# Two one-element PSUM tiles taken ahead of the first head products of an encoder kernel

## The chip, the cores and the metric

The kernel runs on one core of a Trainium2 chip, in one launch. The metric is the device time of one execution in microseconds, the median of several runs. Times inside an execution come from one profiled execution and are counted from its first instruction.

## The reference

Two layers of a bidirectional encoder on 1024 tokens of width 1024, everything in float32. Layer 0 mixes tokens by latent attention, layer 1 by dilated windows; each layer ends with a squared-ReLU MLP. What matters here is the start of layer 0:

```python
def mla_mixer(h, pos, w_in, g_qa, w_qb, g_kva, w_kvb, g_q, g_k, w_o):
    proj = h @ w_in                                   # 1024 -> 384 + 256 + 32
    q_lat = proj[..., :Q_LORA]
    kv_lat = proj[..., Q_LORA:Q_LORA + KV_LORA]
    k_rope = rope(proj[..., Q_LORA + KV_LORA:], pos)
    q = (rms_norm(q_lat, g_qa) @ w_qb).reshape(B, S, MLA_HEADS, MLA_QK)
    kv = (rms_norm(kv_lat, g_kva) @ w_kvb).reshape(B, S, MLA_HEADS, MLA_NOPE + MLA_V)
    ...
    q = rms_norm(q, g_q)
    k = rms_norm(k, g_k)
    o = dense_attention(q, k, v, MLA_QK ** -0.5)
    return o.reshape(B, S, MLA_HEADS * MLA_V) @ w_o
```

## The kernel before

Every float32 product is made of three matmuls on a high and a low part of each operand (`mm3`, L423 to L427). PSUM has 8 banks, and each PSUM tile here fills one bank. PSUM tiles come from pools; a pool is opened for a stage and closed after it, and the next pool takes over the same 8 banks. A tile may be written once the last reader of the tile that held its bank before has finished; this is kept bank by bank (`reuse_waits="tile"`), so a new stage may begin in the free banks while the old stage still reads others. Which bank a tile gets is settled when the program is built. So is the order of each engine's instructions: each engine works through its own list in that order, and waits on semaphores that count what the other engines have finished.

Function `mla` uses three such pools one after the other.

- **`psA`** (L566): the input projection, for eight token tiles `t` of 128 rows. Accumulators `psin` of two kinds: tag `q`, 416 columns (L588, banks 2 to 5), and tag `kv`, which holds two token tiles (banks 6 and 7). `latent(t)` (L594) reads them: two squares on ACT (L597, L598), `rstd` (ACT L112 and L113, DVE L114 to L116), two scalings on DVE (L600, L601) and a copy of the rotary columns `krw` on ACT (L602). `latents` (L605) transposes the latents on PE into `pslt` (banks 0 and 1) and splits them on ACT and DVE (L121, L122) into `latT`. `k_rope` (L620) ends the stage: DVE L623 and L624, and six POOL instructions.
- **`psB`** (L768): the head products, over two halves `hf` of eight heads and eight token tiles `t`. Per step, two tiles `pq` (9 matmuls of 384 columns each) and two `pkv` (6 matmuls of 512 columns each), then squares on ACT (`sq` L791, `sk`, in the trace `sqk`, L793), sums on DVE (L795, L796), `rstd`, scalings into `st` (ACT L801, DVE L802 and L805, POOL L807 and the rope), and a store to DRAM (`qkv`, L814). In the first half the transposes still owed, `pslt`, stand between the steps (L817 to L822). In the second half the first two heads are prepared between the steps: `prep` (transposes `pqk`; the last of them is split by ACT L733 and DVE L734), `rowmax` (matmul `pmx`, DVE maximum L756) and `rowstore` (`pmt`).
- **`psC`** (L840): the attention itself. Tag `s` (`pss`, L853 to L855) has banks 0 to 2, tag `t` (`pmx` and others) banks 3 to 5, tag `av` banks 6 and 7.

Of the kernel before, what the change touches and what calls it, by code (L numbers as in the profile page):

```python
# [41 lines left out]
class K:  # L42
# [496 lines left out]
    def mla(self, xs, ada0, xs1, mods, tail):  # L539


        nc, a, tc = self.nc, self.a, self.tc
# [225 lines left out]
        with tc.tile_pool(name="psB", bufs=8, space=PSUM, reuse_waits="tile") as psp:  # L768
            B = lambda name: psp.tile([P, 512], F32, tag="b", name=self.nm(name))
            raw = None  # L770
            for hf in range(2):
                w = hw[hf]
                for t in range(NT):
# [1629 lines left out]
```

## Time and profile before

| | us |
|---|---|
| runs, median (lowest to highest) | 3236.82 (3232.02 to 3237.32) |
| the profiled execution's own time | 3228.74 |
| its span, first to last instruction | 3227.0 |

The profile gives each engine's busy time (PE is the matmul engine, DVE and ACT the vector and scalar engines, POOL a slower vector engine, SP issues transfers), what an idle engine waited for, and each instruction's start and length. In a timeline row the first number is the start, the second the length, and a bracket gives the idle time ahead of it and what ended it. Matmuls are pipelined, so the length of one overlaps the next: the distance from start to start is what a matmul costs. The granted clock is the share of full speed that PE got. Here the head products stand from 111 to 230 us of the span.

### The profile page before, as it was taken

How to read it: one execution, taken by the hardware profiler on the slowest of the kernel's cores; microseconds unless marked ns; L12 is line 12 of the kernel's file. 1: busy time of each engine (PE TensorE's matmuls, PEld its weight loads, DVE VectorE, ACT ScalarE, POOL GpSimd, SP SyncE). 2: the span in 40 equal slices, each digit the busy share in tenths (PEclk: the TensorE clock that was granted, in tenths of full speed). 3: DMA queues.
4: the chain of work that ended last, by engine and by line, in shares of the span. 5: the costliest groups of instructions: out<-in, count | busy, mean ns of one | idle time of the engine just before them, and what ended most of it. 6: DMA issues, size and time to landing. Idle time of an engine off the chain costs nothing. (4 is left out here: it accounts for less than half of the span.)

```text
span 3227.0 us, 50801 instructions
## 1 busy us (share of the span) xinstructions
PE 3127.3 (97%) x18034; PEld 2645.7 (82%) x18034; DVE 2383.3 (74%) x4243; ACT 1733.2 (54%) x3507; POOL 919.4 (28%) x1226
## 2 busy tenths in 40 slices
PE   6999999999999999989999999999999999999999
PEld 6877677778788788877889999998998888887887
DVE  6677777746987776588757778777888588778566
ACT  5547777754554433543226677667665264444332
POOL 7464556530111100000123445444454001110010
PEclk9999999999999999999999999999999999999999
DMA  5352322253555779544638877888778536448554
GB/s 193 121 190 80 108 84 92 70 167 111 177 200 175 268 220 307 179 148 162 224 125 187 184 179 178 191 190 174 173 165 202 167 106 214 150 152 311 204 190 129
DMA packets 538926, 552.31 MB, mean 171 GB/s; under 512 B 199429, under 2 KB 421042, under 8 KB 538666
## 3 DMA queue, kind: packets, MB, share of 16 engines
q1 hardware_dynamic: 500874, 443.00, 48.4%
q0 software_dynamic: 27360, 91.31, 7.6%
q10 hardware_dynamic: 10432, 14.68, 1.6%
q8 instruction: 144, 2.36, 0.3%
q14 instruction: 116, 0.95, 0.1%
HBM read 376.17 MB, written 132.62 MB: 158 GB/s over the span
## 5 line engine op out<-in xcount | busy, mean ns | idle before, releaser
L426 PE MATMUL psm<-dl,dh 128*128 128x512 f32 x896 | 350.7, 391 | 8.3 <-DVE dl L122 8.2
L425 PE MATMUL psm<-hf,wf 128*128 128x512 f32 x896 | 350.4, 391 | 2.6 <-ACT wf L121 2.6
L426 PE MATMUL psm<-hf,wf 128*128 128x512 f32 x896 | 349.7, 390 | 0.0
L427 PE MATMUL psm<-dh,dl 128*128 128x512 f32 x896 | 349.7, 390 | 0.0
L427 PE MATMUL psm<-hf,wf 128*128 128x512 f32 x896 | 347.2, 390 | 0.4 <-DVE wf L122 0.4
L425 PE MATMUL psm<-dh,dh 128*128 128x512 f32 x896 | 335.9, 392 | 5.2 <-ACT dh L121 5.2
L425 PE MATMUL psproj<-wqkh,hTp 128*128 128x256 f32 x1024 | 302.0, 295 | 0.0
L427 PE MATMUL psproj<-wqkh,hTp 128*128 128x256 f32 x1024 | 290.4, 284 | 0.0
L426 PE MATMUL psproj<-wqkl,hTp 128*128 128x256 f32 x1024 | 290.3, 283 | 0.0
L121 ACT ACTIVATE dh<-ufr 128x1024 fp32r<-128x1024 f32 x112 | 118.3, 1056 | 175.3 <-PE psm L427 50.0
L426 PEld LDWEIGHTS psm<-dl,dh 128*128 128x128 f32 x896 | 168.7, 188 | 46.5 <-DVE dl L122 11.6
L425 PEld LDWEIGHTS psproj<-wqkh,hTp 128*128 128x128 f32 x1024 | 196.6, 192 | 8.5 <-issue 0.4
L425 PEld LDWEIGHTS psm<-dh,dh 128*128 128x128 f32 x896 | 168.5, 189 | 42.7 <-ACT dh L121 7.8
L425 PEld LDWEIGHTS psm<-hf,wf 128*128 128x128 f32 x896 | 168.7, 188 | 40.1 <-ACT wf L121 5.5
L427 PEld LDWEIGHTS psm<-hf,wf 128*128 128x128 f32 x896 | 168.5, 188 | 35.8 <-DVE wf L122 1.2
L426 PEld LDWEIGHTS psm<-hf,wf 128*128 128x128 f32 x896 | 168.7, 188 | 35.0
L427 PEld LDWEIGHTS psm<-dh,dl 128*128 128x128 f32 x896 | 168.8, 188 | 34.6
L426 PEld LDWEIGHTS psproj<-wqkl,hTp 128*128 128x128 f32 x1024 | 196.8, 192 | 0.2 <-DVE wqkl L122 0.2
L427 PEld LDWEIGHTS psproj<-wqkh,hTp 128*128 128x128 f32 x1024 | 196.4, 192 | 0.2
L122 DVE TENSOR_TENSOR dl<-ufr,dh 128x1024 fp32r<-128x1024 f32 x112 | 136.9, 1222 | 77.3 <-ACT dh L121 58.6
L756 DVE TENSOR_REDUCE mx<-pmx 128x1 f32<-128x512 f32 x256 | 165.1, 682 | 29.5 <-PE pmx L754 29.3
L122 POOL TENSOR_TENSOR pl<-p,ph 128x1024 fp32r<-128x1024 f32 x58 | 141.3, 2436 | 138.8 <-ACT ph L121 133.8
(400 smaller groups left out, 8926.4 us busy)
## 6 DMA issues: line engine op xcount, KB each, us to landing
ufr<-uf SPq DMA_DIRECT2D x112, 512.0 KB
adaw<-in_ada_w SPq DMA_DIRECT2D x96, 512.0 KB
w2r<-in_mlp_w SPq DMA_DIRECT2D x96, 512.0 KB
w1r<-in_mlp_w SPq DMA_DIRECT2D x64, 512.0 KB
bt<-bias SPq DMA_DIRECT2D x128, 256.0 KB
wqkr<-in_dil_w_in SPq DMA_DIRECT2D x96, 256.0 KB
qkv<-st SPq DMA_DIRECT2D x32, 512.0 KB
hraw<-qkv SPq DMA_DIRECT2D x32, 512.0 KB
```

The source lines that it names most:

```text
L121: nc.scalar.activation(hi, src, AF.Copy)
L122: (lo_eng or nc.vector).tensor_tensor(lo, src, hi.bitcast(F32), op=ALU.subtract)
L425: mm(out, lh, rh, start=first, stop=False)
L426: mm(out, lh, rl, start=False, stop=False)
L427: mm(out, ll, rh, start=False, stop=last)
L756: nc.vector.tensor_reduce(maxes[h][:, 2 * j + b : 2 * j + b + 1], ps, op=ALU.max, axis=AX.X)
```

## The change

Ahead of the loops of the second stage, two tiles are taken from its pool and one element of each is set to zero by DVE. Nothing reads them. They take the first two banks that the builder hands out, and the products get later ones.

```diff
         with tc.tile_pool(name="psB", bufs=8, space=PSUM, reuse_waits="tile") as psp:
             B = lambda name: psp.tile([P, 512], F32, tag="b", name=self.nm(name))
             raw = None
+            for _ in range(2):
+                nc.vector.memset(B("skip")[0:1, 0:1], 0.0)
             for hf in range(2):
                 w = hw[hf]
                 for t in range(NT):
```

Lines behind it have numbers higher by 2 in the changed kernel (L791 becomes L793). The banks that the builder hands out in the second stage, in the order in which tiles are taken:

| tile | before | after | what held the bank of after in `psA` |
|---|---|---|---|
| the two `skip` | | 0, 7 | `pslt`; `kv` of `t` 6 and 7 |
| `pq`, `pq` of `t` 0 | 0, 7 | 6, 5 | `kv` of `t` 4 and 5; `q` of `t` 5 |
| `pkv`, `pkv` of `t` 0 | 6, 5 | 4, 1 | `q` of `t` 6; `pslt` |
| `pslt`, `pslt` | 4, 3 | 2, 3 | `q` of `t` 4; `q` of `t` 7 |
| `pq`, `pq` of `t` 1 | 2, 1 | 0, 7 | the two `skip` |
| ... | | | |
| `pq`, `pq`, `pkv`, `pkv` of the last step | 3, 7, 1, 4 | 3, 5, 7, 2 | |
| the last `pqk` | 2 | 0 | |

From the first `pq` to the last `pqk` the banks of after are those of before with the numbers exchanged (0, 1, 2, 3, 4, 5, 6, 7 become 6, 7, 0, 3, 2, 1, 4, 5): two tiles that shared a bank before share one now. All other pools have the banks they had, and all tiles in SBUF their addresses.

The order of the instructions on PE, ACT, POOL and SP is the same. On DVE the two memsets stand between the two instructions of the last `k_rope`; the first rows are before, the second after.

```order
L601 TENSOR_SCALAR lat_7109<-psin_6956,lry_7112 128x256
L623 TENSOR_TENSOR krsq_7123<-krw 128x128
L624 TENSOR_REDUCE krss<-krsq_7123 128x4
L795 TENSOR_REDUCE hms_7182<-sq_7180 128x8
L796 TENSOR_REDUCE hms_7182<-sqk_7181 128x8
```

```order
L601 TENSOR_SCALAR lat_7109<-psin_6956,lry_7112 128x256
L623 TENSOR_TENSOR krsq_7123<-krw 128x128
L772 MEMSET skip_7144 1x1
L772 MEMSET skip_7146 1x1
L624 TENSOR_REDUCE krss<-krsq_7123 128x4
L797 TENSOR_REDUCE hms_7186<-sq_7184 128x8
L798 TENSOR_REDUCE hms_7186<-sqk_7185 128x8
```

The memsets are behind the scaling L601 of the last `latent`, and so behind the last reader of both their banks. In the dilated attention of layer 1, one DVE instruction of a `rstd` (`drt`, L114) also stands two rows earlier than before; nothing else differs on DVE.

What PE waits for differs at both ends of the stage. At its beginning, with the semaphores that a row waits for in brackets, before and then after:

```order
L427 MATMUL pq_7144<-whh_7015,latT_6774 128x384
L425 MATMUL pq_7145<-whh_6983,latT_6743 128x384 [waits DVE_49]
L426 MATMUL pq_7145<-whl_6984,latT_6743 128x384
...
L425 MATMUL pkv_7146<-whh_7031,latT_6773 128x512 [waits Activation_49]
L426 MATMUL pkv_7146<-whl_7032,latT_6773 128x512
```

```order
L427 MATMUL pq_7148<-whh_7015,latT_6774 128x384
L425 MATMUL pq_7149<-whh_6983,latT_6743 128x384 [waits PE_49,Activation_49]
L426 MATMUL pq_7149<-whl_6984,latT_6743 128x384
...
L425 MATMUL pkv_7150<-whh_7031,latT_6773 128x512 [waits Activation_49]
L426 MATMUL pkv_7150<-whl_7032,latT_6773 128x512
```

Before, the second `pq` waits for DVE's last scaling L601 of `t` 7, which reads bank 7. After, it waits for ACT's copy L602 of `t` 5, and the first `pkv` for the copy L602 of `t` 6.

At the end of the stage, the first scores of the attention, before and then after:

```order
L853 MATMUL pss_8696<-qh_8131,kh_8129 128x512 [waits DMAHW4_49,DMAHW3_49,DVE_49]
L854 MATMUL pss_8696<-ql_8132,kh_8129 128x512
L855 MATMUL pss_8696<-qh_8131,kl_8130 128x512
L754 MATMUL pmx_8701<-kh_8359,qh_8361 128x512 [waits DVE_49,Activation_49]
L853 MATMUL pss_8697<-qh_8131,kh_8129 128x512 [waits PE_49]
```

```order
L855 MATMUL pss_8700<-qh_8135,kh_8133 128x512 [waits DMAHW4_49,DMAHW3_49,DVE_49]
L856 MATMUL pss_8700<-ql_8136,kh_8133 128x512
L857 MATMUL pss_8700<-qh_8135,kl_8134 128x512
L754 MATMUL pmx_8705<-kh_8363,qh_8365 128x512 [waits DVE_49,Activation_49]
L855 MATMUL pss_8701<-qh_8135,kh_8133 128x512 [waits DVE_49,Activation_49]
```

The first `pss` (bank 0) now waits for DVE L734, which reads the last `pqk`; the second (bank 2) for the last scaling L805 of the stage (L807 of the changed kernel) and ACT's copy beside it. The `pmx` between them (bank 3) waits for the same scaling L802 as before.

## The prediction

> **What bounds the kernel now.** I read the busy times first, then what PE waited for in the whole execution. In a wait row the figures are the total in us, how often, and the longest.
>
> ```profile
> PE 3127.3 (97%) x18034; PEld 2645.7 (82%) x18034; DVE 2383.3 (74%) x4243; ACT 1733.2 (54%) x3507; POOL 919.4 (28%) x1226
> PE pq L425 <- DVE lat L601: 4.0, 1, 4.0
> PE pmt L762 <- DVE nm L761: 2.6, 1, 2.6
> PE pmx L754 <- DVE st L802: 2.3, 1, 2.3
> PE pq L425 <- DVE st L802: 0.9, 1, 0.9
> ```
>
> PE is busy for 97% of the span, so a time that PE loses anywhere is lost at the end, and a stall removed is a gain unless a later wait takes it back. The change touches the banks of one stage, and the first wait row is the one place where that stage waits for the stage before it: one wait of 4.0 us. The other three lie inside the stage or at its end. PE's timeline there:
>
> ```profile
> 111.16 0.34 PE L425 MATMUL pq<-whh,latT 128*128 128x384 f32 x1
> 112.55 0.34 PE L427 MATMUL pq<-whh,latT 128*128 128x384 f32 x1
> 116.86 0.69 PE L425 MATMUL pq<-whh,latT 128*128 128x384 f32 x1 [3.97 <-DVE lat L601]
> 119.88 0.39 PE L425 MATMUL pkv<-whh,latT 128*128 128x512 f32 x1
> 122.65 0.82 PE L612 MATMUL pslt<-ident,lat 128*128 128x128 f32 x6
> 123.22 0.42 PE L425 MATMUL pq<-whh,latT 128*128 128x384 f32 x1
> ```
>
> The first `pq` runs through. The second, in bank 7, stands 3.97 us until DVE has read that bank for the last time. Then its nine matmuls take 119.88 - 116.86 = 3.02 us. The nine of the first `pq` took 1.39 us from the first start to the ninth, 0.174 us each or 1.57 us in all: another 1.45 us is lost. The granted clock says why; in a row of this view it stands behind the engines' busy times, and ahead of the transfers' share and their GB/s:
>
> ```profile
> 112.00:120.00 8.00, 4.03 (x16) 3.71 (x15) 3.46 (x12) 2.59 (x11) 1.79 (x6) 0.79 0.00 0
> 117.00:118.00 1.00, 1.00 (x4) 1.00 (x5) 0.29 (x1) 0.02 (x1) 1.00 (x5) 0.50 0.00 0
> ```
>
> After the stall PE runs at half clock. And there is no transfer between 112 and 120 us. So no queue of transfers carries over the stall, and every later transfer is issued by work behind it.
>
> **The change, part by part.** What the new banks wait for, and what ACT and DVE do meanwhile:
>
> ```profile
> 113.74 0.20 ACT L602 ACTIVATE krw<-psin 128x32 f32<-128x32 f32 x1 [0.87 <-DVE lat L600]
> 116.54 0.48 ACT L791 ACTIVATE sq<-pq 128x384 f32<-128x384 f32 x1
> 121.47 0.39 ACT L793 ACTIVATE sqk<-pkv 128x256 f32<-128x256 f32 x1 [0.90 <-PE pkv L427]
> 121.75 0.38 ACT L801 ACTIVATE st<-pkv 128x256 f32<-128x256 f32 x1
> 122.85 0.38 ACT L793 ACTIVATE sqk<-pkv 128x256 f32<-128x256 f32 x1 [0.72 <-PE pkv L427]
> 125.09 0.49 ACT L791 ACTIVATE sq<-pq 128x384 f32<-128x384 f32 x1
> 125.48 0.93 ACT L562 ACTIVATE whh<-wqr,colc 128x768 fp32r<-128x768 f32 x1
> ```
>
> ```profile
> 108.31 0.69 DVE L122 TENSOR_TENSOR latT<-pslt,latT 128x512 fp32r<-128x512 f32 x1
> 116.33 0.48 DVE L601 TENSOR_SCALAR lat<-psin,lry 128x256 f32<-128x256 f32 x1
> 117.03 0.29 DVE L624 TENSOR_REDUCE krss<-krsq 128x4 f32<-128x128 f32 x1
> 123.26 0.69 DVE L796 TENSOR_REDUCE hms<-sqk 128x8 f32<-128x512 f32 x1 [1.70 <-ACT sqk L793]
> ```
>
> *PE at the beginning.* The first two `pq` take banks whose readers (those of token tiles 4 and 5) stand on DVE and ACT ahead of the split that ends at 109.00. They run from 111.16 to 114.30 without a gap (18 x 0.174 us). The first `pkv` needs bank 4, read for the last time by ACT's `krw` copy, which ends at 113.94: 0.36 us before PE comes. The second `pkv` needs bank 1, a `pslt` split by 109.00. The twelve matmuls take 122.65 - 119.88 = 2.77 us, to 117.07. The six transposes take 0.57 us; they need the last latents, ready at 116.81, and end at 117.64. The next `pq` pair stands behind the memsets, due by 117.2. So this pair starts at 117.64 instead of 123.22: PE is 5.58 us ahead (3.97 + 1.45, the rest rounding).
>
> *ACT and DVE.* ACT's list is in order, and the first `sq` stands behind the last `krw` copy as before: it stays at 116.54. But then everything is there. By the spacing of these same operations (0.39 us for a `sq`, 125.09 to 125.48; 0.28 us for the others, 121.47 to 121.75) the second `sqk` starts at 116.54 + 2 x 0.39 + 2 x 0.28 = 117.88 instead of 122.85. So DVE's sum L796, and all that follows on DVE, POOL and SP, is 4.97 us ahead: 0.6 us less than PE. PE gets back to DVE's pace where it waits for a bank, as in the row of 0.9 us above (PE waits for DVE's `st`). I take 4.97, with 5.58 as the other end.
>
> *The memsets.* The trace has no memset in PSUM. The nearest row is one of 128 elements in SBUF:
>
> ```profile
> L96 DVE MEMSET ones<- 128x1 f32 x1 | 0.1, 59 | 0.0
> L114 DVE SCALAR_TENSOR_TENSOR drt<-dms,dry x96: 152/164/1108, 1679.8 to 2492.7; 128x8 f32<-128x8 f32 x96
> ```
>
> Two take 0.12 us by this row, 0.58 us if each lasted as long as the 0.29 us reduction behind it. They come after L623 and push only L624 and the first sum, which waits for ACT's second `sq` (about 117.4) anyway. I take nothing; the bound is 0 to 0.5 us. They gain nothing either: no one else reads them. The moved `drt` in layer 1 is one instruction of 0.16 us that swaps places with its neighbours: 0, within 0.2 us either way.
>
> *Inside the stage* the exchange of bank numbers keeps every pair of tiles that share a bank, so the waits of 2.6 and 0.9 us stay and only move with the rest.
>
> *The end of the stage*:
>
> ```profile
> 230.44 0.48 PE L853 MATMUL pss<-qh,kh 97*128 97x512 f32 x1
> 233.66 0.47 PE L754 MATMUL pmx<-kh,qh 96*128 96x512 f32 x1 [2.27 <-DVE st L802]
> 233.97 0.40 PE L853 MATMUL pss<-qh,kh 97*128 97x512 f32 x1
> ```
>
> ```profile
> 231.56 0.74 DVE L734 SCALAR_TENSOR_TENSOR ql<-pqk,gq,qh 96x512 fp32r<-96x512 f32 x1
> 234.23 0.41 DVE L805 TENSOR_TENSOR st<-pkv,hry 128x256 f32<-128x256 f32 x1
> ```
>
> In the times of before: the first `pss` now waits until L734 ends, 232.30, and its three matmuls end near 233.1. This is hidden, since the `pmx` behind it still waits for `st` until 233.66. The second `pss` would now wait for L805, which ends at 234.64; with the 0.1 us that PE takes after such an end it starts near 234.7 instead of 233.97. That is 0.6 to 0.75 us late. Part may be made up, since the `pmx` behind it then find their banks free. I take 0.55, between 0 and 0.8.
>
> *Sum*: -4.97 + 0.55 = -4.4 us. The ends: -5.6 + 0 = -5.6, and -4.97 + 0.5 + 0.8 = -3.7. On the profiled execution that is 3228.7 - 4.4 = 3224.3. This execution lies 8.1 us under the median of the runs, 3236.8; the same 4.4 us off that median give **3232.4 us**. The work in between is not touched, and no transfer crosses the stall.
>
> **The clock.** Other stalls also cost clock, but not by a plain rule:
>
> ```profile
> 198.10:201.50 3.40, 1.28 (x6) 1.00 0.61 209
> 201.50:204.90 3.40, 3.30 (x12) 0.54 0.46 154
> 221.94:225.35 3.41, 1.30 (x8) 1.00 0.34 113
> 225.35:228.76 3.41, 3.41 (x20) 1.00 0.17 57
> 235.87:239.28 3.41, 3.41 (x10) 0.50 0.58 208
> ```
>
> ```profile
> core 0: 3227.0 us, clock 0.990
> ```
>
> A stretch with 1.28 us of busy PE was followed by 3.4 us at half clock, a loss of about 1.7 us; one with 1.30 us was not. A mean clock of 0.990 over 3227 us is a loss of 32 us, some 19 such stretches. When all later work moves by 4 to 5 us, each may come or go. The Trainium skill, "TensorE: Matmul & The Clock Gate", Part 1, says that the clock is halved after an idle window of about 3.4 us, that this window runs free of the program, and that it rises again after a busy one. By that rule only the removed stall is long enough to be sure of its slow stretch, and the sum would be the same -4.4; the trace agrees on the 3.97 us stall, but shows one after a stretch with 1.28 us of work in it too.
>
> **The rivals.**
> - *Slow stretches fall away besides* (faster by more than 0.2%). Each takes 1.7 us more: 3230.7 with one, 3229.0 with two. For it: two of the three stalls left in this stage and its end had one. Against it: the same may go the other way, and the runs before, 3232.0 to 3237.3, already average over it. 0.27.
> - *The gain is taken back* at 3236.8, because something at the end of the stage does not move. It would have to be a transfer or an engine not fed by the head products; the row with no transfers between 112 and 120 us speaks against it. 0.13.
> - *Slower, by the same clock*: the first `pss` splits the single wait at the end (2.27 us) into two or three, and more of the stalls that stay, here and in layer 1, are followed by a slow stretch. Three more slow stretches, 5.1 us, cancel the gain; slower by 0.2% takes seven, 3243. Seven of some 19 in one direction is unlikely. 0.05.
> - *The memsets hold up DVE*: only if they stood ahead of L601. They stand behind it, so this is 0.
>
> **How the numbers follow.** The forecast has 0.55. The 0.2% that a measurement can tell from no change is 6.5 us: faster means under 3230.3, slower over 3243.3. The forecast is a gain under that bound. Two stretches less, or one together with the spread of a few us that the runs show, pass it: 0.30 for faster. Slower is 0.05, the rest 0.65. The range goes from two stretches less with some spread, 3227, to the gain taken back with as much, 3238.
>
> **What would show it.** In the changed profile: the wait for L601 at the second `pq` is gone; PE runs from 111 to beyond 118 us without a gap and at clock 1.00; the third `pq` starts near 117.6; the first `sq` stays at 116.5 and the second `sqk` comes at 117.9; the qkv stores and the last `pkv` come about 5 us earlier. At the end a short wait appears ahead of the first `pss` and another ahead of the second. I am wrong if the first `pkv` waits for `krw`, if PE stands at the third `pq` for the memsets, or if the first scores do not come 4 to 5 us earlier.

## The result, and the profile after

| | before | after |
|---|---|---|
| median (lowest to highest), us | 3234.81 (3228.12 to 3238.24), 20 runs | 3229.42 (3222.77 to 3231.61), 20 runs |
| ratio, 95% interval | | 0.9983 (0.9977 to 0.9989) |
| the profiled execution's span, its own time | 3227.0, 3228.74 | 3226.8, 3228.56 |

The change made the kernel 5.4 us faster; by the interval the gain lies between 3.6 and 7.4 us. The two profiled executions differ by 0.2 us only. A single pair of executions can't show a gain of this size: the spans of the ten profiled in this study lie between 3223.1 and 3240.9 us, and one and the same program, before, gave 3227.0 and 3230.8. So the gain is read from the medians, and the traces are read for places: what waits for what, counted from the first `pq` of each execution.

What PE waited for in the changed kernel from 100 to 245 us, five of the eight rows:

```profile
PE pmt L762 <- DVE nm L761: 2.6, 1, 2.6
PE pss L855 <- DVE ql L734: 1.7, 1, 1.7
PE pq L425 <- DVE st L804: 0.9, 1, 0.9
PE pss L855 <- DVE st L807: 0.7, 1, 0.7
PE pmx L754 <- DVE st L804: 0.3, 1, 0.3
```

The 4.0 us wait for L601 is gone. At the exit the single wait of 2.3 us has become three, 1.7, 0.3 and 0.7 us. PE's timeline and two rows of its windows at the entry:

```profile
111.31 0.34 PE L425 MATMUL pq<-whh,latT 128*128 128x384 f32 x1
112.87 0.34 PE L425 MATMUL pq<-whh,latT 128*128 128x384 f32 x1
114.43 0.39 PE L425 MATMUL pkv<-whh,latT 128*128 128x512 f32 x1
117.20 0.82 PE L612 MATMUL pslt<-ident,lat 128*128 128x128 f32 x6
117.77 0.42 PE L425 MATMUL pq<-whh,latT 128*128 128x384 f32 x1
112.00:120.00 8.00, 8.00 (x46) 1.00 0.00 0
200.00:245.00 45.00, 38.77 (x164) 0.89 0.39 130
```

The second `pq` follows the first after 1.56 us. PE is busy for all of the 8 us in which it had 4.03 before, and the granted clock is 1.00 instead of 0.79. The third `pq` stands 6.46 us behind the first, where it stood 12.06 us behind it before. ACT and DVE in the same stretch:

```profile
116.69 0.87 ACT L793 ACTIVATE sq<-pq 128x384 f32<-128x384 f32 x2
117.96 0.43 ACT L795 ACTIVATE sqk<-pkv 128x256 f32<-128x256 f32 x1
117.15 0.06 DVE L772 MEMSET skip<- 1x1 f32 x2
118.46 0.68 DVE L798 TENSOR_REDUCE hms<-sqk 128x8 f32<-128x512 f32 x1
```

The second `sqk` comes 6.65 us after the first `pq`, before it was 11.69. The two memsets take 0.06 us together. At the exit:

```profile
227.69 0.50 PE L855 MATMUL pss<-qh,kh 97*128 97x512 f32 x1 [1.67 <-DVE ql L734]
229.00 0.47 PE L754 MATMUL pmx<-kh,qh 96*128 96x512 f32 x1 [0.33 <-DVE st L804]
230.12 0.76 PE L855 MATMUL pss<-qh,kh 97*128 97x512 f32 x1 [0.66 <-DVE st L807]
```

The second `pss` starts 118.81 us after the first `pq`; before it was 122.81. That is 4.0 us, somewhat less than the entry gained.

PE has the same matmuls in the same order in both kernels, so each can be compared with its counterpart. Counted from the first `pq`, the changed kernel is 3.0 us ahead at the matmul that before starts at 245 us, 3.1 us at the one at 1500 us and 0.3 us at the one at 2000 us. The two spans thus became equal in layer 1, far behind this stage. Two profiled executions of the kernel before drift apart by 3.6 us between the same two points, 1500 and 2000 us, so this loss can't be put down to the change.

### The profile page after: what moved, and what is told of

Its sections match the earlier page's. It is cut to its first block, busy times and chain, and to the rows that moved or that the text cites. A ratio compares the mean times of both kernels' runs of the same rounds, so it can differ in the third digit from the quotient of the medians.

```text
span 3226.8 us, 50803 instructions
## 1 busy us (share of the span) xinstructions
PE 3127.3 (97%) x18034; PEld 2646.7 (82%) x18034; DVE 2384.1 (74%) x4245; ACT 1732.8 (54%) x3507; POOL 920.8 (29%) x1226
## 5 line engine op out<-in xcount | busy, mean ns | idle before, releaser
L756 DVE TENSOR_REDUCE mx<-pmx 128x1 f32<-128x512 f32 x256 | 165.2, 682 | 31.2 <-PE pmx L754 30.9
```

The lines of the kernel that those rows point to most:

```text
L756: nc.vector.tensor_reduce(maxes[h][:, 2 * j + b : 2 * j + b + 1], ps, op=ALU.max, axis=AX.X)
```

## The experiments

All times below are medians, and the ratios are to the kernel before, run beside them on the same chip; a ratio compares the runs round by round and so needn't be the quotient of two medians. Before had 3234.02 us in the first four experiments and 3234.64 us in the other four. The theory as it stood ahead of them: the gain is the wait at the second `pq` with the half clock behind it, cut to the lead of ACT and DVE, less the new wait at the second `pss`. The main rivals: another number of skipped tiles does as well, or what moved the time is the clock, whatever the banks.

### One tile, and three tiles

```diff
-            for _ in range(2):
+            for _ in range(1):
```

> One tile is taken ahead of the products instead of two. The first pq then gets bank 7 (read until DVE's last scaling L601), the second bank 6, the pkv banks 5 and 4. Theory (what counts is how long the bank of each of the first four products is still read by the stage before): PE already stands at the first pq, from 111.2 to 116.9 us, 5.7 us instead of 4.0, with nine matmuls more behind the stall, 1.6 us; the second sqk of ACT comes about 1.6 us later than before (122.85). At the end of the stage the first pss has bank 0 with the last step's first pkv in it and waits until that is read, some 0.9 us later than before. Sum: 1 to 2.5 us slower than the kernel before, 3236 to 3237.5 where before has 3234.8, and about 7 us slower than with two tiles. Rival (the gain comes from turning the banks or from the memsets as such, by whatever means): faster than before, by some part of the 5.4 us that two tiles gave.

Measured: 3240.47 us, ratio 1.0020 (1.0012 to 1.0029), 6.5 us slower than before. The wait moved from the second `pq` to the first and became longer, and the first `pss` waited 3.38 us:

```profile
117.03 0.66 PE L425 MATMUL pq<-whh,latT 128*128 128x384 f32 x1 [5.62 <-DVE lat L601]
238.07 0.74 PE L855 MATMUL pss<-qh,kh 97*128 97x512 f32 x1 [3.38 <-issue]
116.00:118.00 2.00, 0.97 (x3) 0.50 0.00 0
200.00:245.00 45.00, 35.88 (x144) 0.85 0.48 163
```

The direction was right, and the size far too small. In this execution the clock stood at one half for 6.8 us around the longer stall, and at 0.85 in the last stretch, where before had 0.92. The second `sqk` stood 2.6 us later than in the profile of before (125.48 us against 122.85), the last `pqk` 4.0 us (234.09 against 230.08) and the second `pss` 5.9 us (239.89 against 233.97). What of this belongs to the banks and what to the slow stretches of these two executions was not separated. The profile names no releaser for the 3.38 us (`issue`); the reader that the expectation named, DVE's scaling of the last step's first `pkv`, ended at 237.85 us, 0.22 us ahead of the `pss`. A skip of one tile is thus not half of the change; it puts the late bank under the first product.

```diff
-            for _ in range(2):
+            for _ in range(3):
```

> Three tiles are taken ahead of the products. The pq get banks 5 and 4, the pkv 3 and 1. Theory: bank 4 is read by ACT's krw copy of token tile 6 until 113.9 us and bank 3 by that of token tile 7 until 116.7, so PE stands twice for about 1.2 us, at the second pq and at the first pkv, and the second sqk comes at 119.7 instead of 122.85: 3.2 us gained at the beginning, 0.75 us lost at the end (the first pss waits for the last step's first pq, the second for its second pkv). Sum: 2.4 us faster than before, 3 us slower than with two tiles. Rival (any turn of the banks does it): the same 5.4 us as with two tiles. Rival (more memsets cost more): slower than before.

Measured: 3233.10 us, ratio 0.9993 (0.9985 to 1.0002), 0.9 us faster by the medians and 2.3 us by the ratio, near the 2.4 us expected; the interval does not exclude zero. The waits are smaller and more in number, and the exit is worse than with two tiles:

```profile
PE pss L855 <- issue: 2.9, 1, 2.9
PE pq L425 <- ACT krw L602: 1.1, 1, 1.1
PE pkv L425 <- ACT krw L602: 0.9, 1, 0.9
```

No slow stretch followed the waits of 1.1 and 0.9 us: the clock was 1.00 from 112 to 120 us. At the exit, DVE's scaling of the last step's first `pq`, which the expectation named, ended at 233.49 us, 0.10 us ahead of the first `pss`. Of the counts tried, none to three, two is the only one at which no product of the first step waits.

### The same banks by way of the first pool

```diff
-            for _ in range(2):
-                nc.vector.memset(B("skip")[0:1, 0:1], 0.0)
...
+            nc.vector.memset(psp.tile([P, 2, 256], F32, tag="kv", name=self.nm("kvd"))[0:1, 0, 0:1], 0.0)
```

The added line stands at the start of `psA`. One more `kv` tile there turns round which token tiles end in banks 6 and 7; the second stage has the banks of before.

> No tile is taken in the stage of the products: its banks are those of before throughout. Instead one element of a kv tile is set in the stage before, early (behind the transposes of the constants), which makes that stage lay its kv tiles in banks 2 and 3 and its q tiles in 4 to 7. Bank 7, which the second pq takes, is then that of token tile 5, done long before. Theory: no stall at the second pq; PE stands about 1 us at the second pkv (bank 5, the krw copy of token tile 7); the second sqk comes at 118.25 instead of 122.85. The end of the stage is as before. Sum: 4.5 us faster than before, about the same as with two tiles. Rival (the gain needs the turned banks at the end of the stage, or the memsets at this place): the same as before.

Measured: 3230.61 us, ratio 0.9989 (0.9980 to 0.9998), 3.4 us faster by the medians, 3.6 by the ratio. The wait for L601 is gone here too, with no tile skipped in the second stage, and the exit keeps the single wait of before:

```profile
PE pkv L425 <- ACT krw L602: 0.9, 1, 0.9
PE pq L425 <- DVE st L803: 1.7, 2, 0.9
PE pmx L755 <- DVE st L803: 2.3, 1, 2.3
```

So it is the hand-over of one bank that counts, not the two tiles. The wait of 0.9 us for `krw` was part of the expectation. What the expectation lacked is the third row: PE now waits twice for DVE's `st`, where before has one such wait of 0.9 us. That fits the 1 us by which the gain falls short of the 4.5 us expected, but it was not tried apart, and the interval (0.6 to 6.5 us) holds 4.5 us as well.

### The two tiles one step later

```diff
-            for _ in range(2):
-                nc.vector.memset(B("skip")[0:1, 0:1], 0.0)
             for hf in range(2):
...
+                    for _ in range(2 if (hf, t) == (0, 1) else 0):
+                        nc.vector.memset(B("skip")[0:1, 0:1], 0.0)
```

> The two tiles are taken one step later, ahead of the products of t 1 of the first half. The first four products then have the banks of before, and so have all others, since the two tiles take the two banks that the next pq take anyway and give them back. The memsets stand at nearly the same place of DVE's list, one row later. Theory: the stall of 4 us at the second pq stays, the end is as before; 0 us, within 0.2% of before, about 5 us slower than with the two tiles first. Rival (the memsets, or two tiles more in the pool, do it): 5.4 us faster.

Measured: 3234.69 us, ratio 1.0006 (0.9997 to 1.0015): no change. The same two memsets, behind the first four products, leave the wait where it was:

```profile
117.10 0.69 PE L425 MATMUL pq<-whh,latT 128*128 128x384 f32 x1 [3.97 <-DVE lat L601]
117.00:118.00 1.00, 0.90 (x3) 0.50 0.00 0
122.00:123.00 1.00, 1.00 (x5) 0.66 0.00 0
```

The memsets as such do nothing to the time. The clock rows show something else: the first whole microsecond at half clock begins at 116 us and the last ends at 122, and with the parts beside them (0.66 in the last row is 0.68 us at half clock, 0.93 in the microsecond from 115 us is 0.14 us) half clock lasted some 6.8 us, twice as long as the 3.4 us in the profile of before.

### The exit alone

```diff
+                            if (hf, t) == (1, 7):
+                                for _ in range(1):
+                                    nc.vector.memset(B("skip")[0:1, 0:1], 0.0)
```

These lines stand ahead of the last preparation of the second head; the entry is that of before.

> The banks at the beginning as before; one tile is taken and one element of it set to zero ahead of the last preparation of the second head, so that the last pqk lies in bank 0, where the first pss follows it. Theory (the exit costs nothing at its first wait): the 4.0 us wait for L601 stays; the first pss gets a wait of 1.6 to 1.9 us for DVE's L734, the wait of the pmx behind it shrinks from 2.3 to 0.3 to 0.5 us and ends where it did, so the time is that of before, within 1 us. Rival (the first wait is not hidden, since the two stalls invite one more slow stretch): 1 to 3 us slower than before.

Measured: 3234.43 us, ratio 0.9998 (0.9990 to 1.0007). The waits of its trace:

```profile
PE pq L425 <- DVE lat L601: 4.0, 1, 4.0
PE pss L856 <- DVE ql L734: 1.7, 1, 1.7
PE pmx L754 <- DVE st L802: 0.3, 1, 0.3
```

The new first wait at the exit is hidden: it takes 1.7 us out of the 2.3 us wait behind it, and costs nothing that these runs can tell. The other wait that the changed kernel has at the exit, 0.7 us at the second `pss`, is not in this run. The rival, 1 to 3 us slower, has the upper end of the interval (2.3 us) left to it and no sign in the median. This profiled execution did have a slow last stretch (clock 0.78 from 222 to 245 us); the next two experiments show what that is worth as evidence.

### Both kernels once more

> The changed kernel once more. Theory (slow stretches of the clock come and go between executions): the same waits at the same places, 1.7, 0.3 and 0.7 us at the exit, but a lost clock time from 111 to 245 us that differs from the 4.95 us of the first profile by 1 us or more; 4.4 to 5.4 us faster than before. Rival (the split of the last wait always brings two slow stretches): the same 4.95 us, the exit again at half clock for some 6 us.

> The kernel before once more. Theory: the waits of the first profile (4.0, 2.6, 2.3, 0.9 us) to 0.1 us, a slow stretch behind the 4.0 us wait as there, and others that may differ; a ratio of 1 to the kernel before within 0.1%. Rival (the first profile's 5.3 us of lost clock time are fixed by the program): 5.3 us again.

Measured: changed again 3230.82 us, ratio 0.9988 (0.9979 to 0.9997), 3.8 us faster, by the interval 1.0 to 6.8, where 4.4 to 5.4 were expected; before again 3236.57 us, ratio 1.0003 (0.9993 to 1.0013). The waits were those of the first profiles to 0.1 us, but the clock was not. The windows from 222 to 245 us, in this order: before, before again, changed, changed again.

```profile
222.00:245.00 23.00, 18.68 (x81) 0.93 0.53 177
222.00:245.00 23.00, 17.07 (x82) 1.00 0.58 193
222.00:245.00 23.00, 20.33 (x81) 0.84 0.48 161
222.00:245.00 23.00, 19.15 (x87) 1.00 0.49 161
```

Of 23 us, 1.6 were lost to the clock in one execution of before and none in the other, 3.7 in one of the changed kernel and none in the other (the length times one minus the clock). From 111 to 245 us, added up microsecond by microsecond, both first profiles lost 5.1 us, changed again 1.7 and before again 3.4. So the split wait does not always bring a long slow stretch, and the rival of each expectation falls. Whether it makes one more likely, two executions can't show. The two executions at full clock share another thing, first before again, then changed again:

```profile
240.12 0.50 PE L754 MATMUL pmx<-kh,qh 96*128 96x512 f32 x1 [0.95 <-DVE mx L756]
234.77 0.50 PE L754 MATMUL pmx<-kh,qh 96*128 96x512 f32 x1 [1.17 <-DVE mx L756]
```

The first profiles have no such wait there. Of all ten, the other two without a slow stretch between 226 and 245 us, with three tiles and with the tiles a step later, have it too (1.15 and 0.93 us), and the six with one have at most 0.38 us of it. At full clock PE runs into DVE's maximum L756, so a slow stretch at the exit costs less than the clock time it takes.

### A version with one wait less

```diff
+                    if (hf, t) == (1, 7):
+                        rowstore(0, B("pmt"))
...
-                            if t == 6:
-                                rowstore(0, B("pmt"))
```

This is the changed kernel with one step moved; the added lines stand between the `pq` and the `pkv` products of the step.

> The changed kernel, with the row store of the first head moved from the end of step 6 of the second half to between the pq and the pkv products of step 7. Theory (what is left at the exit is waits that other work can fill): the wait of 2.6 us at pmt goes, since PE has the 18 matmuls of the two pq to do meanwhile, and the first scores come about 2.6 us earlier than in the changed kernel; the row's way over DRAM still ends ahead of the first score that needs it. 2.6 us faster than the changed kernel, 7 to 8 us faster than before. Rival (DVE and ACT set the pace there, not PE): the wait comes back at the first pss or the pmx behind it, and the time is that of the changed kernel, within 1 us.

Measured: 3225.04 us (3222.60 to 3228.74, 5 runs), ratio 0.9966 (0.9954 to 0.9979): 9.6 us faster than before, by the interval 6.8 to 14.9. The changed kernel beside it had 3230.82 us, more than the slowest of these five runs, so the rival, a time within 1 us of it, falls. The timeline of PE:

```profile
220.22 0.27 PE L762 MATMUL pmt<-ident,nm 128*8 128x128 f32 x1
225.48 0.50 PE L855 MATMUL pss<-qh,kh 97*128 97x512 f32 x1 [1.80 <-DVE ql L734]
227.43 0.50 PE L754 MATMUL pmx<-kh,qh 96*128 96x512 f32 x1 [0.98 <-DVE st L806]
227.77 0.40 PE L855 MATMUL pss<-qh,kh 97*128 97x512 f32 x1
```

No wait stands at `pmt`, and the first `pss` waits for the split L734, not for the row that comes back from DRAM. The first `pss` comes 114.15 us after the first `pq`, instead of 116.38 and 116.19 in the two profiles of the changed kernel; the second 116.44 us instead of 118.81 and 118.63. So 2.0 to 2.4 us of the 2.6 us arrive, and the rest turns into the longer wait at the `pmx` (0.98 instead of 0.33 us), where DVE sets the pace. The medians differ by more, 5.8 us; with five runs, and a spread of 6 us in them, that surplus stays unexplained.

## Why the prediction was right, and where it was off

The forecast was 4.4 us less, 3232.4 us from a median of 3236.8. Measured were 5.4 and, in the repeat, 3.8 us less. The median of before came out 2.0 us lower over 20 runs than in the ones that the forecast had, so the absolute time says less than the difference.

- **PE at the beginning**: right. The forecast had PE ahead by 5.58 us; the third `pq` is 5.60 us nearer to the first. The first `pkv` did not wait for `krw`, nor the third `pq` for the memsets. The 0.16 us that the forecast called rounding has another source: idle time is counted from the modelled end of the last matmul, and from start to start the stall cost 4.14 us (116.86 - 112.55 - 0.17), not 3.97.
- **ACT and DVE as the lead that counts**: right for the first step, and wrong for what follows from it. The first `sq` stayed behind the last `krw` copy (116.69 us), and the second `sqk` came at 117.96 us, forecast 117.88 with a first `pq` 0.15 us earlier: a lead of 5.04 us. But PE did not fall back to that lead. In the next step ACT waits for PE in both kernels, and so takes over PE's lead. The rows are of before and of after in turn: the second `sqk` of the next step, the 0.9 us wait at which the forecast expected the fall, and the first `pqk`:

```profile
129.42 0.38 ACT L793 ACTIVATE sqk<-pkv 128x256 f32<-128x256 f32 x1 [0.72 <-PE pkv L427]
123.97 0.38 ACT L795 ACTIVATE sqk<-pkv 128x256 f32<-128x256 f32 x1 [0.72 <-PE pkv L427]
148.91 0.41 PE L425 MATMUL pq<-whh,latT 128*128 128x384 f32 x1 [0.86 <-DVE st L802]
143.48 0.41 PE L425 MATMUL pq<-whh,latT 128*128 128x384 f32 x1 [0.86 <-DVE st L804]
184.44 1.03 PE L729 MATMUL pqk<-ident,hraw 128*96 128x128 f32 x8
179.00 0.60 PE L729 MATMUL pqk<-ident,hraw 128*96 128x128 f32 x4
179.79 0.61 PE L729 MATMUL pqk<-ident,hraw 128*96 128x128 f32 x4 [0.18 <-DMA hraw<-qkv]
```

  Counted from the first `pq`, the leads are 5.60, 5.58 and 5.59 us. Then 0.3 to 0.5 us were lost at the last row, where the profile has PE wait for data read back from DRAM. The repeat of the changed kernel has a wait at the same place (0.29 us), but so has the run with the tiles a step later (0.34 us), whose early banks are those of before; the runs don't show that it belongs to the change.
- **The size of the lead**: this is the term that was mis-sized. The 4.97 us were the wait and the half clock of one execution, cut by a step that did not happen. Four profiled executions with the 4.0 us wait at the second `pq` have the second `sqk` 11.69, 11.85, 12.90 and 12.92 us after the first `pq`; the three with the two tiles at the beginning have 6.64 to 6.66 us, 5.0 to 6.3 us less. By the third `pq`, PE's lead, it is 5.6 to 6.8 us. The wait was 3.97 us in each of the four. What varies is the half clock around its end. The first two rows are of before's repeat, the other two of the exit experiment:

```profile
117.00:118.00 1.00, 0.08 (x1) 0.90 0.00 0
121.00:122.00 1.00, 1.00 (x5) 0.89 0.00 0
115.00:116.00 1.00, 0.00 (x0) 0.89 0.00 0
122.00:123.00 1.00, 1.00 (x4) 0.69 0.00 0
```

  All microseconds between the two rows of a pair are at 0.50. A clock of 0.90 in one microsecond is 0.2 us at half clock, so half clock lasts from 117.8 to 121.2 us in the one, 3.4 us, and from 115.8 to 122.6 us in the other, 6.8 us. The profile that the forecast had showed the cheapest of the four.
- **The exit**: right in its places, and sized at its upper end. Three waits came where they were put. The first is hidden (alone it measured 0). The second leaves PE idle for 0.66 us, but from the `pmx` to the second `pss` it is 1.12 us from start to start instead of 0.31, so the `pss` is 0.8 us late, forecast 0.55 between 0 and 0.8. No run tried this wait apart. The two repeats, both at full clock here, agree: between the last `pqk` and the second `pss` the lead falls from 5.2 to 4.4 us. One sign of being wrong was put too simply: the first `pss` comes only 2.9 us earlier (116.38 us after the first `pq` instead of 119.28), because of the very wait that the forecast had put there; the `pmx` behind it comes 4.8 us earlier.
- **The memsets**: right at nothing; 0.06 us for both, half of the nearest row's 0.12, since the two overlap, and no change when they stand a step later.
- **The sum again**: 5.6 to 6.8 us at the entry, less 0 to 0.5 at the first `pqk` and 0.8 at the exit, give 4.3 to 6.0 us. Both medians' intervals (-3.6 to -7.4, -1.0 to -6.8) hold all of it. That the forecast's 4.4 us lies in it is partly luck: the entry was taken too small, and so were the two losses behind it. Whether a part is given back behind the exit can't be told from these traces, whose spread there is as large as the gain.
- **The rivals**: that the gain is taken back did not happen. Slow stretches did come and go, but the repeats show that they do so in both kernels, and tie them to no edit at the exit. That they "fall away besides" is in the end true of one place alone, the second half-clock stretch that follows the removed stall in two of four executions.

The Trainium skill, "TensorE: Matmul & The Clock Gate", Part 1, has the clock rise only after a busy window of about 3.4 us, and the windows run free of the program. The traces agree: in the exit experiment PE came back 1.2 us after half clock had begun and worked for 2.2 us of the first 3.4, and a second 3.4 us followed; in before's repeat it came back 0.1 us after the beginning, and one length was all. What the prediction took from this section, that the removed stall is long enough to be sure of its slow stretch, does not follow from windows that run free: none need fall whole into 3.97 us. All four executions had the slow stretch all the same. It began 2.7 to 3.9 us after PE had stopped, so the 3.4 us ahead of it were not always idle throughout: in the exit experiment they begin at 112.4 us, and PE worked until 113.0. There the measurement differs from the idle window that the prediction names.

## What to carry to other kernels

When one pool takes over the banks of another, look at which bank the first products get and who reads it last: here a wait there cost the wait itself and the slow clock around its end, and one dummy tile more or less moved it. When PE gains a larger lead than the engines that consume its products, the smaller lead need not be the gain: here ACT and DVE had been standing idle for PE, and took over its lead in the next step. So follow a lead through the next waits of the stage before cutting it. A price that includes half clock should be read as a range (here 3.4 or 6.8 us around the same stall), because a single profile shows one case of it.

## What the runs showed of the hardware that was not expected

- Half clock around the same stall, 3.97 us in each of four executions, lasted about 3.4 us in two and about 6.8 us in two; the second `sqk`, which hangs on it, came 1.1 to 1.2 us later in the latter. The two short ones are executions of the kernel before, the two long ones of experiments whose edits act only behind the stall.
- It can begin while PE still waits. In the exit experiment PE stopped at 113.0 us (3.97 us ahead of 116.97 us), and half clock began at 115.8 us, after 2.8 us.
- Waits of 1.1 and 0.9 us close together were followed by no slow stretch (clock 1.00 from 112 to 120 us with three tiles).
- A memset of one element in PSUM is recorded with 59 ns on DVE, as is the one of 128 elements in SBUF; the two of the changed kernel overlap and take 0.06 us together.
